# A decoder step with routed experts: the first LayerNorm's rows are reloaded unscaled and finished in the last stage, and more expert weights are prefetched

## The chip, the cores and the metric

The kernel runs on one core of one Trainium2 chip. The metric is the device time of one execution in microseconds (us), as the median of several runs; lower is better. The core has five engines, each with an instruction queue of its own: TensorE (PE, matmuls; its weight loads are shown as PEld), VectorE (DVE), ScalarE (ACT), GpSimd (POOL) and SyncE (SP). Sixteen DMA engines serve all queues. Here SP issues almost all weight loads, and a transfer that SP has to wait for holds up everything that SP issues behind it.

## The reference

One layer of a hybrid decoder for 512 prompt rows and 32 sample rows (8 sequences of 4 tokens), all in float32, model width 1024. The mixers (a matrix memory, sliding-window attention, their projections and gates) come first and are not touched by the change. What matters here stands behind them:

```
x = layer_norm(DN_ALPHA * x + mix, ln_g[0], ln_b[0])                        # LN1
x = layer_norm(DN_ALPHA * x + hier_moe(x, ...), ln_g[1], ln_b[1])           # LN2
ple = jax.nn.sigmoid(x @ w_pg) * (p_i @ w_pp)
x = layer_norm(DN_ALPHA * x + ple, ln_g[2], ln_b[2])                        # LN3
```

`hier_moe` routes each row: the best of 4 groups, and in it the best 2 of 8 experts, whose outputs are added with weights. An expert is `silu(x @ w_eg) * (x @ w_eu) @ w_ed`, with w_eg and w_eu of 1024 x 512 and w_ed of 512 x 1024, 6 MiB together. LN1's output x is needed three times: by the router, by the experts, and in the residual sum of LN2. Its scale and shift (ln_g[0], ln_b[0]) are the last step of it.

## The kernel before, in words

**Order of the work.** The mixers end with the output projection, a stream of matmuls over weights that pass through a staging pool on the right side of SBUF. Then come LN1 and the router's logits, the routing (some 17 us of short VectorE operations, with TensorE computing the embeddings `p_i @ w_pp` in between), the expert stage (`expert_phase`, written with semaphores by hand), and the last stage: LN2, the gate projection with `w_pg`, and LN3, one tile of 128 rows after the other (`moe_norm`, `turn`, `embed_norm`), with the 32 sample rows handled apart (`moe_norm_q`, `embed_norm_q`). Within a stage the compiler's scheduler orders the instructions, and `tc.issue_after` puts an instruction behind another. `expert_phase` is a critical section: the engines enter it when what they share has landed, and leave it together (L164), when each has signalled `fin`.

**LN1's rows.** `ln_scale` normalises a tile of rows in place in `r_p` (or `r_s` for the sample rows) without scale and shift, and SP writes it to `x1d` in DRAM. The router and the experts fold scale and shift into their own weights or into the copies behind the transposes, and read `x1d`. For LN2's residual sum, VectorE also multiplies by the gain and adds the shift in place (`ln_affine`, L1689, and `affine` inside the expert stage, L429), two operations a tile, and SP writes those rows to a second array `x1a`. The rows have to leave `r_p`, because it is the place of one expert's w_ed.

**The expert stage.** Four slots hold one expert's weights each: 2 MiB for the first half of gate and up (semaphore `gu`), 2 MiB for the second (`gv`), and 2 MiB for down in two halves (`wd`, `we`). The rows of an expert are worked on in items of 32. The slot of an expert is refilled as TensorE is done with its parts (`gh`, `gu`, `dn`), by a loop on SP that goes through the experts in order (L127 gate and up, L133 down). Some parts of the first four experts are loaded before the stage (`prefetch(slot, which)`); the rest at its start: SP issues a part of slot 3 and slot 2 there, between the writes of `x1a`, and waits for these writes (`xo`) where they leave the place `r_p` to w_ed. When an expert is the last in its slot, SP loads what the last stage needs into the place (`late`, L215): in this order of slots, rows of LN1 into slot 3's `r_p`, half of `w_pg` into slot 0, and the rows of ln_g and ln_b (`gb_rows`) into slot 1.

**The start of the last stage.** GpSimd gathers the two expert outputs of each row from `ybuf` (`gather`). TensorE spreads gains and shifts of LN2 and LN3 over the partitions: a matmul of one identity column, broadcast, with `gb_rows`, 512 columns at a time, and ScalarE copies the result out (`spread`, L2014 and L2015, eight matmuls). ScalarE and VectorE split `w_pg` into two parts (`split_from`). Then `moe_norm(0)` and `turn(0)` (transposes) come, and so on.

## Time and profile before

| what | value |
|---|---|
| median of 3 runs | 1167.32 us (1164.56 to 1167.94) |
| the profiled execution's own time | 1164.36 us |
| its span, from the first to the last instruction | 1162.6 us |
| TensorE busy | 90% of the span, mean granted clock 0.962 |
| VectorE, ScalarE, GpSimd busy | 42%, 28%, 20% |
| moved by DMA | 280.06 MB, mean 241 GB/s |

The span is shorter than the execution's time by what lies around it. Shares of busy time are averages over stages with different limits; what a stage waits for is read from its own windows. A matmul's end is modelled, so a busy TensorE is not one at its peak. [...]

### The profile page before, as it was taken

What the parts mean: (1) busy time and instruction counts of PE and PEld (TensorE: products, weight loads), DVE (VectorE), ACT (ScalarE), POOL (GpSimd) and SP (SyncE); (2) the same over time, 40 slices, a digit from 0 to 9 for tenths busy, and PEclk for the clock granted to TensorE, in tenths of its full rate; (3) what the DMA queues carried; (4) which work ended last, traced back from release to release, by engine and by line L of the source; (5) the groups of instructions that cost most, each with busy time, mean ns of one, the idle gap of its engine ahead of it and who ended that gap; (6) DMA issues with size and microseconds to landing.
All of it is one profiled execution on the core that took longest, in us unless ns stands there. A gap on an engine that the chain in (4) does not pass through costs nothing.

```text
span 1162.6 us, 26684 instructions
## 1 busy us (share of the span) xinstructions
PE 1042.6 (90%) x10267; PEld 810.4 (70%) x10268; DVE 494.1 (42%) x1244; ACT 324.0 (28%) x663; POOL 232.5 (20%) x325
## 2 busy tenths in 40 slices
PE   6999999999999999999999884685998979985986
PEld 6988999999877779889988442342555535542665
DVE  3645533456545546465565620110111111111796
ACT  4411223232554745233212210110222112211411
POOL 4000001301445553104200210110121101111421
PEclk9999999999999999999999998988999989998798
DMA  8542543335214434563496799999999999998901
GB/s 253 145 132 62 156 120 98 78 94 157 71 48 149 130 110 139 167 179 101 160 414 246 289 368 414 418 423 415 421 417 417 417 418 421 415 418 332 341 19 59
DMA packets 113751, 280.06 MB, mean 241 GB/s; under 512 B 15478, under 2 KB 71644, under 8 KB 99824
## 3 DMA queue, kind: packets, MB, share of 16 engines
q1 hardware_dynamic: 92704, 240.06, 55.3%
q0 software_dynamic: 15280, 33.59, 8.3%
q10 hardware_dynamic: 5696, 5.43, 1.5%
q8 instruction: 48, 0.79, 0.3%
q14 instruction: 23, 0.19, 0.1%
HBM read 249.21 MB, written 31.80 MB: 242 GB/s over the span
## 4 chain that ended last, share of the span: by engine, by line
PE 65%; DMA 13%; SPq 12%; DVE 5%; issue 4%; POOL 1%; ACT 0%; ACTq 0%; DVEq 0%; POOLq 0%
PE pj L611 13%; PE pj L613 13%; PE pj L612 12%; PE psG L282 7%; SPq L127 7%; DMA gu<-in_w_eu_dram 4%; SPq L133 4%; DMA w2b<-in_w_eu_dram 4%; PE psY L296 4%; PE tp L1220 2%; DMA x1a<-r_p 1%; PE sp L1266 1%; PE nm L1254 1%; DMA raw<-in_w_a_dram 1%; PE sp L671 1%
## 5 line engine op out<-in xcount | busy, mean ns | idle before, releaser
L611 PE MATMUL pj<-xH,wH 128*128 128x256 f32 (+1 forms) x672 | 198.2, 295 | 0.0
L613 PE MATMUL pj<-xH,wL 128*128 128x256 f32 (+1 forms) x672 | 197.6, 294 | 0.0
L612 PE MATMUL pj<-xL,wH 128*128 128x256 f32 (+1 forms) x672 | 195.8, 291 | 0.0
L524 ACT CAST wH<-raw 128x1024 fp32r<-128x1024 f32 x76 | 79.6, 1048 | 235.9 <-PE pj L612 149.0
L611 PEld LDWEIGHTS pj<-xH,wH 128*128 128x128 f32 x672 | 126.5, 188 | 6.3 <-issue 4.9
L613 PEld LDWEIGHTS pj<-xH,wL 128*128 128x128 f32 x672 | 126.5, 188 | 4.7 <-issue 4.3
L612 PEld LDWEIGHTS pj<-xL,wH 128*128 128x128 f32 x672 | 127.1, 189 | 2.7 <-issue 2.2
L525 DVE TENSOR_TENSOR wL<-raw,wH 128x1024 fp32r<-128x1024 f32 x76 | 94.9, 1249 | 72.6 <-ACT wH L524 71.9
L282 PE MATMUL psG<-w,xT 128*32 128x256 f32 x1216 | 78.2, 401 | 29.2 <-DMA w<-in_w_eu_dram 15.8
L386 ACT ACTIVATE sg<-psG 128x128 f32<-128x128 f32 x50 | 13.9, 278 | 288.2 <-PE psG L282 288.2
L282 PE MATMUL psG<-gu,xT 128*32 128x256 f32 x1088 | 70.7, 403 | 24.4 <-DMA gu<-in_w_eu_dram 18.3
L417 DVE COPY hT<-psH 128x128 f32<-128x128 f32 x50 | 14.6, 292 | 182.6 <-PE psH L287 182.6
L282 PEld LDWEIGHTS psG<-w,xT 128*32 128x32 f32 x1216 | 40.3, 114 | 58.2 <-issue 38.0
L282 PEld LDWEIGHTS psG<-gu,xT 128*32 128x32 f32 x1088 | 35.9, 114 | 50.9 <-issue 29.1
L246 POOL DMA_DIRECT2D ybuf<-ysb x50 | 35.1, 704 | 149.9 <-DVE ysb L424 145.8
L1242 POOL TENSOR_SCALAR lg<-lg,sm 128x256 f32<-128x256 f32 (+1 forms) x64 | 56.0, 888 | 28.6 <-DVE sm L1239 17.4
L412 DVE COPY xT<-xg 128x256 f32 (+1 forms) x50 | 14.7, 294 | 102.1 <-PE psG L282 101.8
L373 ACT ACTIVATE xg<-psX,gcol 128x128 f32 (+1 forms) x100 | 36.4, 468 | 47.0 <-PE psX L275 47.0
L282 PE MATMUL psG<-w2a,xT 128*32 128x256 f32 x448 | 32.2, 427 | 19.1 <-DMA w2a<-in_w_eu_dram 14.1
L611 PE MATMUL pj<-wH,xH 128*128 128x256 f32 x160 | 47.4, 296 | 0.0
L613 PE MATMUL pj<-wH,xL 128*128 128x256 f32 x160 | 44.9, 280 | 0.0
L612 PE MATMUL pj<-wL,xH 128*128 128x256 f32 x160 | 44.8, 280 | 0.0
(578 smaller groups left out, 2188.5 us busy)
## 6 DMA issues: line engine op xcount, KB each, us to landing
w<-in_w_eg_dram SPq DMA_DIRECT2D x28, 1024.0 KB, 22.6
w<-in_w_eu_dram SPq DMA_DIRECT2D x28, 1024.0 KB, 24.3
w<-in_w_ed_dram SPq DMA_DIRECT2D x28, 1024.0 KB, 25.3
raw<-in_w_in_dram SPq DMA_DIRECT2D x22, 1024.0 KB
w2b<-in_w_ed_dram SPq DMA_DIRECT2D x14, 1024.0 KB, 25.0
gu<-in_w_eg_dram SPq DMA_DIRECT2D x12, 1024.0 KB, 23.7
gu<-in_w_eu_dram SPq DMA_DIRECT2D x12, 1024.0 KB, 26.1
r_p<-in_w_ed_dram SPq DMA_DIRECT2D x12, 1024.0 KB, 22.9
```

Of the source, the lines that this page charges most:

```text
L127: return [eng.dma_start(out=W[s][half][:, i], in_=w[i][bass.ds(e, 1)].rearrange("a (p k) f -> (a p) k f", p=P)[:, ks]) for i in range(2)]
L133: return eng.dma_start(out=W[s][2][:, ks], in_=w[2][bass.ds(e, 1)].rearrange("a (k p) d -> p (a k) d", p=P)[:, ks])
L246: gp.dma_start(out=ybuf[bass.ds(i1 * 32, 32)].rearrange("t (c d) -> c t d", c=4), in_=ysb[:, r]).then_inc(S[f"y{r}"], 16)
L282: m = pe.matmul(psG[32 * q:32 * q + 32], xT[:, k], W[s][half][:, :, kh, P * q:P * q + P], start=k == 0, stop=k == KD - 1)
L296: m = pe.matmul(psY[32 * q:32 * q + 32], hT[:, 32 * k:32 * k + 32], W[s][2][:, k, 256 * q:256 * q + 256], start=k == 0, stop=k == 3)
L373: m = act.activation(out=out, in_=psX[:, k], func=AF.Identity, bias=gcol[:, 1, k:k + 1], scale=gcol[:, 0, k:k + 1])
L524: act.copy(out=H, in_=src)
L525: return eng.tensor_tensor(out=L, in0=src, in1=H.bitcast(F32), op=ALU.subtract)
L611: pe.matmul(out, lh(k), rh(k), start=start and i == 0, stop=False)
L612: pe.matmul(out, lh(k), rl(k), start=False, stop=False)
L613: pe.matmul(out, ll(k), rh(k), start=False, stop=stop and i == len(ks) - 1)
L1242: gp.tensor_scalar(out=lg[:, par, j, 0:nk], in0=lg[:, par, j, 0:nk], scalar1=sm[:, 2, par, j:j + 1], scalar2=None, op0=ALU.mult)
```

## The change

- `x1a` and all writes of it go. `late` reloads all four tiles of rows from `x1d`, unscaled, in the expert stage's end (semaphore `rb`); before, one came back there and three in the last stage. VectorE's scale and shift of these rows move behind the experts: two tiles at the end of the expert stage, one early in the last stage, one (and the sample rows) in the middle of it.
- The two tiles `w2b` and `gu3` (8 rows of 1024 a partition each) become four of half the size, so that each waits for its own part of the staging pool alone. Of the first four experts everything but the second half of slot 3's gate and up is prefetched before the stage: 3 MiB more than before. SP's issues at the stage's start shrink to that one pair.
- Four of the six spreads (LN1's and LN2's gains and shifts, eight matmuls) are made inside the expert stage, by TensorE behind its last matmul, with ScalarE copying; LN3's two stay in the last stage.
- Small index and weight computations move from the last stage into the routing. Two runs of idle matmuls stand in the last stage, six become eight in the routing. The second half of `w_pg` is issued behind the first gather's landing. `moe_norm_q` and `embed_norm_q` come earlier.

```diff
-def expert_phase(tc, pool, psum, ident, meta, tok, x1, W, w, ybuf, spare, gcol, gb, xs, xa, late, warm):
...
+def expert_phase(tc, pool, psum, ident, meta, tok, x1, W, w, ybuf, spare, gcol, late, rows, spreads, xs, any_):
...
-        def rows_out(t):
-            sp.dma_start(out=xa[t * P:(t + 1) * P], in_=xs[t]).then_inc(S["xo"], 16)
-
-        rows_out(0)
         for d in load_gu(sp, W, NB - 1, w, NB - 1, 1):
             d.then_inc(S[f"gv{NB - 1}"], 16)
-        sp.wait_ge(S["xo"], 16)
-        load_dn(sp, W, NB - 1, w, NB - 1, 0).then_inc(S[f"wd{NB - 1}"], 16)
-        for t in (1, 2):
-            sp.wait_ge(S["af"], 2 * t)
-            rows_out(t)
-        load_dn(sp, W, NB - 2, w, NB - 2, 1).then_inc(S[f"we{NB - 2}"], 16)
-        sp.wait_ge(S["xo"], 48)
-        load_dn(sp, W, NB - 1, w, NB - 1, 1).then_inc(S[f"we{NB - 1}"], 16)
...
-                        for out, src in late[s]:
-                            sp.dma_start(out=out, in_=src).then_inc(S["al"], 16)
+                        for out, src, name in late[s]:
+                            sp.dma_start(out=out, in_=src).then_inc(S[name], 16)
...
-        sp.wait_ge(S["al"], 16 * sum(len(loads) for loads in late))
+        of = lambda which: 16 * sum(name == which for loads in late for _, _, name in loads)
+        sp.wait_ge(S["al"], of("al"))
...
-        for s in range(NB - 1):
-            for n in ("wd", "we")[:1 + (s < NB - 2)]:
+        for s in range(NB):
+            for n in ("wd", "we"):
...
+        halves = [(n, out[:, 512 * i:512 * (i + 1)], which, slice(512 * i, 512 * (i + 1))) for n, (out, which) in enumerate(spreads)
+                  for i in range(2)]
+        banks = [psX[:, 4 * i:4 * i + 4].rearrange("p k t -> p (k t)") for i in range(2)]
+        pe.wait_ge(S["gr"], 32)
+        for n, (_, _, which, cs) in enumerate(halves):
+            if n > 1:
+                pe.wait_ge(S["sc"], n - 1)
+            pe.matmul(banks[n % 2], ident[0:6, which:which + 1].to_broadcast([6, P]), rows[:, cs], start=True, stop=True).then_inc(S["se"], 1)
...
+        for n, (_, out, _, _) in enumerate(halves):
+            act.wait_ge(S["se"], n + 1)
+            act.copy(out=out, in_=banks[n % 2]).then_inc(S["sc"], 1)
+        act.wait_ge(S["sc"], len(halves))
...
-        def affine(t, i):
-            if i:
-                dve.wait_ge(S["af"], 2 * t - 1)
-            dve.tensor_tensor(out=xs[t], in0=xs[t], in1=gb[:, i], op=(ALU.mult, ALU.add)[i]).then_inc(S["af"], 1)
-
-        affine(1, 0)
...
-        affine(1, 1)
-        affine(2, 0)
-        affine(2, 1)
...
+        dve.wait_ge(S["rb"], of("rb"))
+        for i, op in enumerate((ALU.mult, ALU.add)):
+            dve.wait_ge(S["sc"], 2 * i + 2)
+            if i:
+                dve.wait_ge(S["ra"], len(xs))
+            for x in xs:
+                dve.tensor_tensor(out=x, in0=x, in1=spreads[i][0], op=op).then_inc(S["ra"], 1)
+        dve.wait_ge(S["ra"], 2 * len(xs))
...
+    spart = stg.tile([P, 256], F32, name="spart", bufs=1)
...
-    w2b = WB.tile([P, 8 * D], F32, name="w2b")
-    w_tiles[2] = (w_tiles[2][0], halves_of(w2b[:, 0:4 * D])[0], w2b[:, 4 * D:].rearrange("p (k d) -> p k d", k=4), None)
-    gu3 = WB.tile([P, 8 * D], F32, name="gu3")
-    w_tiles.append((*halves_of(gu3), r_p, None))
-
-    wpp, pT = gu3[:, 4 * D:6 * D].rearrange("p (k d) -> p k d", k=2), gu3[:, 6 * D:6 * D + 2 * NG].rearrange("p (k s) -> p k s", k=2)
+
+    gu3a, gu3b, w2b, w2d = (WB.tile([P, 4 * D], F32, name=name) for name in ("gu3a", "gu3b", "w2b", "w2d"))
+    w_tiles[2] = (halves_of(w2a)[0], halves_of(w2b)[0], w2d[:].rearrange("p (k d) -> p k d", k=4), None)
+    w_tiles.append((halves_of(gu3a)[0], halves_of(gu3b)[0], r_p, None))
+    for _ in prefetch(2, (1,)):
+        pass
+
+    wpp, pT = gu3b[:, 0:2 * D].rearrange("p (k d) -> p k d", k=2), gu3b[:, 2 * D:2 * D + 2 * NG].rearrange("p (k s) -> p k s", k=2)
...
-    gb1 = ln_consts(w_tiles[2][2][:, 2:4], 0, act)
-    for _ in prefetch(2, (1,)):
-        pass
-    next(prefetch(2, (2,)))
...
-    def ln_affine(t, parts=(0, 1)):
...
-    def x1_out(t):
-        sy.dma_start(out=x1a[t * P:t * P + x1s[t].shape[0]], in_=x1s[t])
...
-        logit = dve.tensor_tensor(out=lgt[:rows, t], in0=pl[:rows, t], in1=brr[:rows], op=ALU.add)
-        if t in (1, 2):
-            with tc.issue_after(logit.ins):
-                ln_affine(NT, (t - 1,))
-    for _ in prefetch(3, (0,)):
-        pass
-    x1_out(NT)
+        dve.tensor_tensor(out=lgt[:rows, t], in0=pl[:rows, t], in1=brr[:rows], op=ALU.add)
+    for s, which in ((2, 2), (3, 0), (3, 2)):
+        for _ in prefetch(s, (which,)):
...
-        PL = pool("pl", bufs=4, stack=scope)
+        PL = pool("pl", bufs=3, stack=scope)
...
-        with tc.issue_after(tokens.ins):
-            ln_affine(0)
-            x1_out(0)
-            ln_affine(1)
+
         idle = rps([P, 512], "pj", 2)
         with tc.issue_after(product.ins):
-            for _ in range(6):
-                pe.matmul(idle[:, 0:256], ident, keep[:, 0:256], start=True, stop=True)
+            for _ in range(8):
+                product = pe.matmul(idle[:, 0:256], ident, keep[:, 0:256], start=True, stop=True)
+        with tc.issue_after(tokens.ins):
+
+            dve.tensor_scalar(out=wsum, in0=wts[:, 1], scalar1=1.0, scalar2=ALPHA, op0=ALU.add, op1=ALU.mult)
...
+            pq = rps([P, 4], "nm")
+            with tc.issue_after(product.ins):
+                pe.matmul(pq, same[:NS].rearrange("p q t -> p (q t)"), smp4, start=True, stop=True)
...
-    gain2, shift2, gain3, shift3 = (row(W1, i) for i in range(4))
-
-    gb_rows = row(W1, 4)[0:4]
-    gbq = row(W1, 4).rearrange("p (i j d) -> p i j d", i=2, j=2)
+    gain1, shift1, gain2, shift2 = (row(W1, i) for i in range(4))
+    gain3, shift3 = row(W1, 11), row(w2a, 2)
+
+    gb_rows = row(W1, 4)[0:6]
+
...
-    r_back = lambda t: (r_p[:, t], x1a[t * P:(t + 1) * P])
+    r_back = lambda t: (r_p[:, t], x1d[t * P:(t + 1) * P])
     late = [
-        [pg_half(0)],
-        [(gb_rows[2 * j:2 * j + 2], A[n][0, 1:3]) for j, n in enumerate(("ln_g", "ln_b"))],
+        [(*pg_half(0), "al")],
+        [(gb_rows[3 * j:3 * j + 3], A[n][0], "gr") for j, n in enumerate(("ln_g", "ln_b"))],
         [],
-        [r_back(0)],
+        [(*r_back(t), "rb") for t in range(NT)],
     ]
+    spreads = [(gain1, 0), (shift1, 3), (gain2, 1), (shift2, 4)]
...
+    def keep_busy(n, behind=None):
+
+        idle = ps2.tile([P, 256], F32, name="pp", bufs=1)
+        with tc.issue_after(behind.ins) if behind else nullcontext():
+            for _ in range(n):
+                m = pe.matmul(idle, ident, keep[:, 0:256], start=True, stop=True)
+        return m
+
+    def affine(x, gain, shift):
+        dve.tensor_tensor(out=x, in0=x, in1=gain, op=ALU.mult)
+        return dve.tensor_tensor(out=x, in0=x, in1=shift, op=ALU.add)
...
-        return ln_apply(x2, stats, gain2, shift2)
+        if t:
+            return ln_apply(x2, stats, gain2, shift2)
+        for half in range(2):
+            cs = slice(512 * half, 512 * (half + 1))
+            first = ln_apply(x2[:, cs], stats, gain2[:, cs], shift2[:, cs])
+        return first
...
+        affine(x1q, gbq[0][:, 0], gbq[0][:, 1])
...
     gather(1)
 
-    for out, src in (pg_half(1), r_back(1), (embeds[:, 0:512], pld[P:2 * P, 512:]), r_back(2), (embeds[:, 512:512 + D], pld[2 * P:3 * P]),
...
-        sy.dma_start(out=out, in_=src)
-    spreads = chain(spread(gain2, 0), spread(shift2, 2), spread(gain3, 1), spread(shift3, 3))
+    for n, (out, src) in enumerate((pg_half(1), (embeds[:, 0:512], pld[P:2 * P, 512:]), (embeds[:, 512:512 + D], pld[2 * P:3 * P]),
+                                    (embeds[:, 512 + D:], pld[3 * P:4 * P]), (pls, plsd[:]),
+                                    (x1q, x1d[SEQ:].rearrange("t (q d) -> q t d", q=4)))):
+        with tc.issue_after(first.ins) if n else nullcontext():
+            dma = sy.dma_start(out=out, in_=src)
+        if n == 0:
+            first = dma
+            tc.add_manual_dep(dma.ins, landed.ins.name, mybir.DependencyInfo(mybir.DependencyClass.Sync, mybir.DependencyReason.DATA),
+                              reason="behind the first rows")
+    busy = keep_busy(8)
     for k in range(KD):
-        copied = next(spreads) if k >= 4 else None
-        with tc.issue_after(copied.ins) if copied else nullcontext():
-            split_from(pg(k, 0, 0, 512), pg(k, 1, 0, 512), pg_in[0][:, k])
-    for copied in spreads:
-        pass
-
-    idle = ps2.tile([P, 256], F32, name="pp", bufs=1)
-    with tc.issue_after(spread_last["ins"].ins):
-        for _ in range(6):
-            pe.matmul(idle, ident, keep[:, 0:256], start=True, stop=True)
+        cast = split_from(pg(k, 0, 0, 512), pg(k, 1, 0, 512), pg_in[0][:, k])
+    with tc.issue_after(busy.ins), tc.issue_after(cast.ins):
+        third = affine(x1s[2], gain1, shift1)
+        spread(gain3, 2)
+        busy = spread(shift3, 5)
+    keep_busy(8, busy)
...
+    with tc.issue_after(third.ins):
+        behind, applied = moe_norm(0)
...
-            with tc.issue_after(applied.ins if t > 1 else lows.ins):
-                if t < NT:
+            if t < NT:
+                with tc.issue_after(applied.ins if t > 1 else lows.ins):
+                    if t == NT - 1:
+                        affine(x1s[t], gain1, shift1)
                     behind, applied = moe_norm(t)
-                else:
+            if t == NT - 2:
+                with tc.issue_after(applied.ins):
                     moe_norm_q()
-        if t > NT:
-            embed_norm_q()
+            if t == NT:
+                embed_norm_q()
```

## Rows read from the trace of the kernel before

**Rows 1.** Window of 100 us: length, busy times, PE clock, DMA share, GB/s.
```profile
800.00:900.00 100.00, 87.42 (x1394) 50.10 (x1390) 17.06 (x57) 20.33 (x50) 14.69 (x22) 0.97 1.02 419
```

**Rows 2.** DMA issues of SP as the expert stage starts.
```profile
681.59 0.38 SPq L133 DMA_DIRECT2D r_p<-in_w_ed_dram  x1
684.45 0.37 SPq L127 DMA_DIRECT2D w<-in_w_eg_dram  x1
```

**Rows 3.** Timeline of TensorE, first items.
```profile
668.16 3.66 PE L282 MATMUL psG<-w,xT 128*32 128x256 f32 x64
...
679.98 1.91 PE L296 MATMUL psY<-w,hT 128*32 128x256 f32 x32
...
711.66 3.64 PE L282 MATMUL psG<-w,xT 128*32 128x256 f32 x32 [7.50 <-DMA w<-in_w_eu_dram]
```

**Rows 4.** Waits of SP, 655 to 1067 us: total, times, longest.
```profile
SPq L164 <- DMA xg<-x1d,tok: 3.6, 1, 3.6
...
SPq L164 <- DMA x1a<-r_p: 1.0, 1, 1.0
```

**Rows 5.** Timeline of VectorE behind the routing.
```profile
653.47 4.62 DVE L1689 TENSOR_TENSOR r_p<-r_p,w2b 128x1024 f32<-128x1024 f32 x4
```

**Rows 6.** A window of 4 us behind the prefetches of the routing.
```profile
652.00:656.00 4.00, 3.35 (x18) 1.72 (x18) 3.60 (x8) 0.00 (x0) 2.37 (x3) 1.00 0.46 175
```

**Rows 7.** Late DMA issues of SP as the expert stage ends.
```profile
1045.03 0.42 SPq L215 DMA_DIRECT2D r_p<-x1a  x1
1050.23 0.39 SPq L215 DMA_DIRECT2D w<-in_w_pg_dram  x1
1062.42 0.31 SPq L215 DMA_DIRECT2D w<-in_ln_g_dram  x1
```

**Rows 8.** Windows behind the last expert matmuls.
```profile
1068.00:1069.00 1.00, 0.00 (x0) 0.00 (x0) 0.00 (x0) 0.00 (x0) 0.54 (x1) 1.00 0.39 150
...
1071.00:1072.00 1.00, 0.00 (x0) 0.00 (x0) 0.00 (x0) 0.00 (x0) 0.00 (x0) 0.50 0.02 8
```

**Rows 9.** Timeline of TensorE from the last expert matmul on.
```profile
1064.69 1.93 PE L296 MATMUL psY<-w2b,hT 128*32 128x256 f32 x32 [1.01 <-DVE hT L417]
1072.84 13.98 PE L2014 MATMUL po<-w,keep 4*128 4x512 f32 x16 [6.22 <-SPq L164]
...
1086.76 5.00 PE L2117 MATMUL pp<-keep 128*128 128x256 f32 x12
...
1091.59 1.04 PE L2034 MATMUL tp<-keep,r_p 128*128 128x128 f32 x8
...
1134.79 1.03 PE L2034 MATMUL tp<-keep,r_p 128*128 128x128 f32 x8
```

**Rows 10.** Windows while TensorE runs spreads, then idle matmuls.
```profile
1080.00:1084.00 4.00, 4.00 (x5) 1.40 (x5) 2.31 (x4) 2.24 (x4) 0.00 (x0) 0.50 1.04 420
...
1088.00:1092.00 4.00, 4.00 (x14) 3.21 (x14) 1.28 (x1) 0.00 (x0) 3.37 (x3) 0.61 1.01 411
```

**Rows 11.** Timelines of VectorE, GpSimd, ScalarE, and one chain line.
```profile
1067.85 3.85 DMA ybuf<-ysb
...
1073.53 1.03 POOL L1999 DMA_INDIRECT w<-ybuf,yidx  x1 [4.99 <-SPq L164]
...
1075.27 1.88 DVE L525 TENSOR_TENSOR pg<-w,pg 128x512 fp32r<-128x512 f32 x3
...
1083.74 1.28 DVE L2020 SCALAR_TENSOR_TENSOR r_p<-w,wts,r_p 128x1024 f32<-128x1024 f32 x1 [0.68 <-DMA w<-ybuf,yidx]
...
1086.86 0.59 ACT L2015 COPY w<-po 128x512 f32<-128x512 f32 x1 [1.12 <-PE po L2014]
...
1092.85 1.29 DVE L2036 TENSOR_TENSOR xT<-tp,xT 128x512 fp32r<-128x512 f32 x2 [3.12 <-issue]
...
1128.88 1.27 DVE L1683 SCALAR_TENSOR_TENSOR r_p<-r_p,lmv,w 128x1024 f32<-128x1024 f32 x1
```

90 lines of the change are left out of this document (40 added, 50 removed).

## The prediction

> **What bounds the kernel now.** I read the page first, then windows over the whole span, and then, for the stages that the change touches, SP's queue, TensorE's timeline, the waits and the windows again in fine steps. Through the expert stage the DMA engines are full: in the window shown, and in the others from 690 to 1060 us, their share is 1.02 at about 419 GB/s, while TensorE is at 87% [rows 1]. TensorE waits there for weights, not the weights for TensorE. So that stage is a stream of bytes: it ends earlier by what its start comes earlier and by what is taken out of it. Behind it the bound changes: the end of the stage waits for a store, the start of the last stage for gathers, VectorE and a TensorE at half clock, and its rest for VectorE and TensorE in turn.
>
> **Part 1: the stream of weights starts earlier.** Before, slot 0's second expert is first asked for at 684.45 us, because SP stood until 681.59 waiting for the writes of LN1's rows, and then read its registers for 2.5 us (684.45 less 681.59 and 0.38) [rows 2]. Now SP has one pair to issue at some 663.5 us and is at that point by about 667.5. What then holds it is TensorE: the first 32 of the 64 matmul records of the first item are through at 668.16 + 3.66/2 = 670.0, the others at 671.8 [rows 3]. So 4 MiB (4.19 MB) are asked for at 670 to 672 us, and take 10.0 us at 419 GB/s. The down part is free at 679.98 + 1.91 = 681.9 [rows 3], just as these are through. From there the queue never empties. When the old stream started, 684.45, the new one is ahead by those 10.0 us and by 684.45 - 681.9 = 2.5 us: 12.5. TensorE can't take all of it at once: its second item in slot 1 waited only 7.5 us [rows 3]. What it can't take stays in the queue as lead, and the next items wait for their own landings again, so the last weights land 12.5 us earlier.
>
> To this comes the entry into the stage. It waited for the first gather, and then 1.0 us more for a write of `x1a` [rows 4]. Without the write it can begin some 0.8 us earlier, behind the gather and the index matmul moved there. Together **13.3 us** off. Bounds: 10 (entry 2 us later through more traffic, the down part 1 us later) and 15 (the gather lands another 1.5 us earlier, as four VectorE operations of 4.62/4 = 1.16 us that stood behind the token list are gone [rows 5]).
>
> The prefetches that make it possible cost no time where they land before the entry. By the sizes they put about 2 MB more into the time in front of it (3 MiB of weights, less 1 MiB of gains and shifts), 5 us at 419 GB/s, and the old queue ran empty inside 652 to 656 us [rows 6]: some 658 us, in front of an entry at 661.5. If that cover is gone, each us is a us. The small operations moved into the routing stand behind the token list and in front of the same gather: nothing, bound 0.5 us.
>
> **Part 2: the end of the stage gets longer.** This is the term that I think is easily overlooked. The spreads now run behind the last expert matmul, which ends at 1064.69 + 1.93 = 1066.6 (times of this part are before's; all of them move by part 1), and the stage isn't left until all eight are copied. They need `gb_rows`, which SP asks for last, at 1062.42, behind the rows at 1045.03 and 2 MiB of `w_pg` at 1050.23 [rows 7]. Before, this queue is through by 1068.4: the DMA share falls to 0.39 in that us, and what follows is the last store [rows 8]. Now three more tiles of rows, 1.57 MB, are in front: 3.75 us, so 1072.1, and 1.3 us until the semaphore is seen, an estimate between 0.5 and 3: 1073.4.
>
> By then TensorE has been idle for 6.8 us. Its granted clock is down to 0.50 from 1071 on in the same idle time of before [rows 8], and the eight spreads of before, begun cold at 1072.84, took 13.98 us, with the clock at 0.50 in the window shown and in its neighbours [rows 9, 10]. I take the same 13.98 us. Then come the last copy, 0.59 [rows 11], and the way out of the stage, 0.9 (before, the last store landed at 1067.85 + 3.85 = 1071.7, and the spreads began 1.1 later [rows 9, 11]). 1073.4 + 14.0 + 0.6 + 0.9 = 1088.9, against 1072.8: **16.1 us** on. Behind TensorE's new wait for `gb_rows` stand only the spreads and its `fin`, but ScalarE, VectorE, SP and GpSimd all wait for these. The four VectorE operations on two tiles, 4 x 1.16 [rows 5], and the reload of the rows are hidden under the spreads; if the spreads were short, they would be next, at about 1076 us. Bounds: 15 and 18 by the landing; 11.4 if the clock rises (a rival).
>
> [...]
>
> **Part 3: the last stage begins quicker.** Before, from the stage's end at 1072.8, the first transposes start at 1091.59, 18.8 us later, and the second half of `turn(0)` is through at 1092.85 + 1.29 = 1094.1, 21.3 later [rows 9, 11]. Eight spreads and idle matmuls to 1091.8 kept TensorE until then [rows 9], and the second gathered tile landed at 1083.7, among 2 MiB of `w_pg` and three tiles of rows [rows 11]. Now four spreads are left, and `w_pg`'s second half waits for the gather. SP's new wait for that gather holds the other half of `w_pg`, the embeddings and the sample rows behind it; at 419 GB/s the 2 MiB of `w_pg` take 5 us and are there by some +15, in front of the splits that need it at +18, and the rest is needed later: nothing, bound 1 us. VectorE is what sets the pace: from +1.0 it has eight subtractions of 1.88/3 = 0.63 (5.0), then the third tile's two operations (2.3): +8.3. The gathered tiles should be there by +8 (the first is issued at +0.7 [rows 11]). The first sum takes 1.2, to +9.5. From the second sum to the first transposes it was 1091.59 - 1083.74 = 7.85, with about 1.9 of waiting for idle matmuls in it: 5.95. The halves of tile 0 save 0.6: transposes at +14.9, and the second half through at +17.9. **3.4 us** off; bounds 1 (the tiles land as late as before) and 4.5.
>
> Behind it, work is only reordered up to the fourth tile. VectorE gains two operations (2.3 us) and the sample rows' part, which I estimate at 4 us from its operations on a quarter of the columns, in front of the fourth tile's LN2. That ended at 1128.88 + 1.27 = 1130.15, and TensorE turned to it at 1134.79 [rows 9, 11]: 4.6 us of cover for 6.4. The 1.8 us left over can be filled by the sample rows' matmuls, which now come earlier. I take nothing, bounds -1.7 and +4.6.
>
> **The sum.** -13.3 + 16.1 - 3.4 = -0.6 us, on the profiled execution's 1164.36: 1163.8. The median of the runs is 2.96 above that execution, so in its terms 1166.7. About 0.3% (3.5 us) is what a measurement of this kernel can tell from no change.
>
> **Rivals.**
> - *The clock rises under the spreads* (0.14). For it: idle matmuls of 128 rows, begun at 1086.76 at the same half clock, had it at full by about 1091, as the window's mean of 0.61 shows [rows 9, 10]. Against it: 14 us of 4-row matmuls didn't. If it rose as late as there, 2.5 spreads would run at 1.75 us and 5.5 at half of that: 9.2 instead of 14.0, and the time is 1161.9.
> - *`gb_rows` lands before TensorE is done* (0.05), because small transfers get past the large ones. The spreads then follow warm, 7 us, and the rows' operations end the stage near 1076: part 2 is 3.5, and the time 1154.
> - *The favourable ends add up* (0.13): the stage entered 1.5 us earlier, the matmuls of the sample rows in a gap (-1.7), tiles landing early (-1): 1162.5.
> - *VectorE becomes late in the middle of the last stage* (0.13), the one on the other side. If the fourth tile's LN2 is late by all of 6.4 us behind a scheduler's order that puts the sample rows first, the 4.6 us of cover are needed elsewhere and TensorE stands: +4.6, 1171.3. It decides from 4.1 us on.
> - *The stage isn't entered earlier* (0.09), so that the change doesn't do what it says: the place of slot 3's down part is free only when the rows' writes are out, and these now queue behind more weights. If its 2 MiB land at 665 instead of 658, the entry is 4 us later than I count: 1170.7. It decides from 661.5 on.
>
> **How the numbers follow.** The forecast, no change that can be told, has 0.46, with 1166.7 and 1163.2 to 1170.2 of its own. The first three rivals are faster by more than 0.3%, 0.32; the last two slower, 0.22. The range leaves out about one in ten on either side: 1158 (early entry together with a rising clock) to 1171.5.
>
> **What would show it.** Part 1: SP asks for slot 0's second expert near 670 us, and TensorE's last expert matmuls start near 1051.4 instead of 1064.69. Part 2: eight spreads of some 14 us at a clock of 0.50 between the last expert matmul and the first gather, that begin 6 to 7 us after TensorE's last. Part 3: first transposes 15 us behind the stage's end. I am wrong if the spreads run at 1.00, if they begin right behind the last matmul, or if the stream starts later than 673 us.

## The result: 0.6% slower

The changed kernel takes 1174.74 us (median of 16 runs, 1169.1 to 1176.77), the kernel before 1167.39 beside it (16 runs): a ratio of 1.0058 (95%: 1.0044 to 1.0073), which is 6.8 us of 1167.39, and outside the range that was given. Its profiled execution is the median one: own time 1174.74, span 1173.1. That is 10.5 us above the span of before; as before's profiled execution is 3 us below its median, sums made between these two executions come out some 3 us too high.

Two views of SP in the changed kernel come first: its issues around the stage's start and end, and the wait that was new (total, times, longest).

```profile
668.14 0.36 SPq L127 DMA_DIRECT2D w<-in_w_eg_dram  x1
...
1053.88 1.69 SPq L202 DMA_DIRECT2D w<-in_ln_g_dram  x1
1055.61 0.39 SPq L202 DMA_DIRECT2D w<-in_ln_b_dram  x1
1089.17 0.40 SPq L2119 DMA_DIRECT2D w<-in_w_pg_dram  x1
```
```profile
SPq L2119 <- DMA w<-ybuf,yidx: 8.1, 2, 7.5
```

Slot 0's second expert is asked for at 668.14, 16.3 us earlier than in [rows 2] (forecast 670). From there on the transfer engines stay busy, as foreseen: in windows of 2 us from 672 to 700 us their share is 0.97 or more. Windows of the changed kernel, in the expert stage and behind it (length, busy times, TensorE's clock as a share of full speed, DMA share, GB/s):

```profile
800.00:900.00 100.00, 93.20 (x1531) 53.39 (x1527) 18.87 (x63) 20.92 (x51) 16.07 (x24) 1.00 1.02 410
1062.00:1064.00 2.00, 0.00 (x0) 0.00 (x0) 0.00 (x0) 0.00 (x0) 0.00 (x0) 0.50 0.59 219
1066.00:1081.00 15.00, 14.01 (x16) 4.97 (x16) 4.72 (x4) 4.69 (x8) 0.00 (x0) 0.50 0.00 0
```

The first one answers to [rows 1], and this is the line that the prediction didn't have: the DMA share is 1.02 as before, but what these full engines moved is 410 GB/s, not 419. It is so through the whole stage (413 from 720 to 800 us, 412 from 900 to 1050). TensorE's timeline of the same kernel, from the last expert matmul on, answers to [rows 9]:

```profile
1056.15 1.93 PE L284 MATMUL psY<-w2d,hT 128*32 128x256 f32 x32 [1.01 <-DVE hT L418]
1066.35 14.01 PE L360 MATMUL psX<-w,keep 6*128 6x512 f32 x16 [8.26 <-DMA w<-in_ln_b_dram]
1081.73 5.58 PE L2017 MATMUL pp<-keep 128*128 128x256 f32 x16 [1.37 <-SPq L163]
1087.25 3.77 PE L2008 MATMUL po<-w,keep 6*128 6x512 f32 x8
...
1096.44 1.32 PE L2046 MATMUL tp<-keep,r_p 128*128 128x128 f32 x8 [1.77 <-DVE r_p L1676]
...
1114.68 1.94 PE L2046 MATMUL tp<-keep,r_p 128*128 128x128 f32 x8 [5.46 <-DVE r_p L1676]
```

From slot 0's request to the last expert matmuls it was 1064.69 - 684.45 = 380.2 us before and is 1056.15 - 668.14 = 388.0 now. The stage's weights therefore end 8.5 us earlier, not 13.3. Behind them TensorE waits 8.26 us for the rows of ln_g and ln_b, and the eight spreads take 14.01 us at a clock of 0.50. The last stage starts 1081.73 - 1056.15 = 25.58 us behind the last expert matmuls, before 1072.84 - 1064.69 = 8.15: 17.4 on, forecast 16.1. The first transposes stand 14.7 us behind the last stage's start, forecast 14.9. The whole last stage is 1173.1 - 1081.73 = 91.4 us long, before 1162.6 - 1072.84 = 89.8: 1.6 on, where 3.4 off was forecast. Sum: -8.5 + 17.4 + 1.6 = 10.5.

What lowers the rate? In the middle of the stage the engines do the same transfers of the same sizes, but into other places of SBUF, where each tile of weights has 128 partitions. Part of the change, seen above only as its uses, moves small tiles out of and into the pool `const`, which lies in front of the large ones:

```diff
-    trib = const.tile([P, P], BF16, name="trib")
-    oneb = const.tile([P, P], BF16, name="oneb")
-    one = const.tile([P, 2, NEXP], F32, name="one")
-    lgt = const.tile([P, NT5, NGRP + NEXP], F32, name="lgt")
+    trib = RC.tile([P, P], BF16, name="trib")
...
+    wsum = const.tile([P, NT5], F32, name="wsum")
+    yidxq = const.tile([P, 2], I32, name="yidxq")
+    smpq = const.tile([P, 4], F32, name="smpq")
+    same = const.tile([P, 4, NS], F32, name="same")
+    quarter = const.tile([P, 4], F32, name="quarter")
+    which = const.tile([P, 4], F32, name="which")
```

By the addresses in the two built programs, 832 bytes a partition less lie in front of `r_p`, `w0`, `w1` and `w2a`. Before, these began at bytes 12544, 29952, 79104 and 128256 of each partition, all 256 past a multiple of 512; now at 11712, 29120, 78272 and 127424, all 64 short of one. The tiles on the right side (`w2b`, `w2d`, `gu3a`, `gu3b`; before `w2b`, `gu3`) begin 480 past a multiple of 512 in both kernels.

### The profile page after: what moved, and what is told of

Same layout as the page of the kernel before. It is cut to its first block, busy times and chain, and to the rows that moved or that the text cites. A ratio compares the mean times of both kernels' runs of the same rounds, so it can differ in the third digit from the quotient of the medians.

```text
span 1173.1 us, 26748 instructions
## 1 busy us (share of the span) xinstructions
PE 1051.4 (90%) x10299; PEld 816.5 (70%) x10300; DVE 493.3 (42%) x1246; ACT 326.6 (28%) x667; POOL 229.1 (20%) x325
## 4 chain that ended last, share of the span: by engine, by line
PE 64%; DMA 16%; SPq 12%; DVE 5%; issue 2%; ACT 0%; POOL 0%; DVEq 0%; ACTq 0%; POOLq 0%
PE pj L612 13%; PE pj L614 12%; PE pj L613 12%; SPq L127 8%; DMA w2b<-in_w_eu_dram 6%; PE psG L270 6%; DMA gu3b<-in_w_eu_dram 4%; SPq L133 3%; PE psY L284 3%; PE tp L1221 2%; PE sp L1267 1%; PE nm L1255 1%; PE psX L360 1%; DMA raw<-in_w_a_dram 1%; PE sp L672 1%
## 5 line engine op out<-in xcount | busy, mean ns | idle before, releaser
L270 PE MATMUL psG<-w,xT 128*32 128x256 f32 x1216 | 74.8, 387 | 22.6 <-issue 11.7
L383 ACT ACTIVATE sg<-psG 128x128 f32<-128x128 f32 x50 | 13.9, 278 | 281.3 <-PE psG L270 281.3
L418 DVE COPY hT<-psH 128x128 f32<-128x128 f32 x50 | 14.6, 292 | 170.9 <-PE psH L275 170.9
L413 DVE COPY xT<-xg 128x256 f32 (+1 forms) x50 | 14.7, 295 | 109.7 <-PE psG L270 109.4
L270 PE MATMUL psG<-gu3a,xT 128*32 128x256 f32 x544 | 35.9, 407 | 20.9 <-DMA gu3a<-in_w_eu_dram 14.9
L270 PEld LDWEIGHTS psG<-gu3a,xT 128*32 128x32 f32 x544 | 19.5, 116 | 35.3 <-issue 29.1
## 6 DMA issues: line engine op xcount, KB each, us to landing
w<-in_w_ed_dram SPq DMA_DIRECT2D x28, 1024.0 KB, 25.2
r_p<-in_w_ed_dram SPq DMA_DIRECT2D x12, 1024.0 KB, 23.4
```

The source lines that it names most:

```text
L270: m = pe.matmul(psG[32 * q:32 * q + 32], xT[:, k], W[s][half][:, :, kh, P * q:P * q + P], start=k == 0, stop=k == KD - 1)
```

## The experiments

Medians in us, with the ratio to the kernel before, run on the same chip beside them. "To stage" goes from the start of the last expert matmuls to the last stage's first matmul, and "last stage" from there to the span's end; these and the rate are of one profiled execution. No kernel here leaves out a part of the computation.

| run | median | ratio (95%) | GB/s, 800 to 900 us | to stage | last stage |
|---|---|---|---|---|---|
| before | 1167.39 | | 419 | 8.2 | 89.8 |
| after | 1174.74 | 1.0058 (1.0044 to 1.0073) | 410 | 25.6 | 91.4 |
| e0, one run | 1165.86 | | 419 | 8.1 | 89.7 |
| e4 | 1168.23 | 0.9993 (0.9977 to 1.0009) | 418 | 25.2 | 92.4 |
| e5 | 1175.1 | 1.0058 (1.0042 to 1.0074) | 412 | 8.2 | 90.1 |
| e8 | 1165.25 | 0.9968 (0.9951 to 0.9985) | 420 | 21.8 | 91.9 |
| e2 | 1166.63 | 0.9982 (0.9964 to 1.0001) | 411 | 14.6 | 91.9 |
| e3 | 1181.61 | 1.0102 (1.0076 to 1.0129) | 411 | 31.0 | 93.2 |
| e6 | 1163.94 | 0.9962 (0.9949 to 0.9975) | 411 | 10.6 | 93.4 |
| e1 | 1177.39 | 1.0068 (1.0043 to 1.0093) | 411 | 24.5 | 93.7 |
| e11 | 1175.27 | 1.0061 (1.004 to 1.0081) | 411 | 23.9 | 92.2 |
| e7 | 1177.34 | 1.0065 (1.0046 to 1.0085) | 412 | 24.0 | 91.7 |
| e12 | 1164.66 | 0.9976 (0.9958 to 0.9994) | 420 | 22.6 | 92.9 |
| e15 | 1164.03 | 0.9975 (0.9961 to 0.9989) | 420 | 23.4 | 88.3 |
| e9 | 1153.81 | 0.9867 (0.984 to 0.9895) | 420 | 10.6 | 92.2 |

### Where the weights lie (e0, e4, e5, e8)

e0 is the kernel before, unchanged, to see how far its stream's rate repeats.

> The kernel before, unchanged, for its weight stream. The changed kernel's stream ran at 410 to 413 GB/s in the windows from 720 to 1050 us, that of before at 418 to 419; over 360 us that is some 6 us. If the change slows the stream, this run shows 418 to 419 again, while the changed kernel's relatives run with it show 410 to 413. The rival, that the rate belongs to the chip or the run, gives the same rate in all kernels of this call.

e4 is the changed kernel with one tile 64 bytes longer, of which the old part alone is used. The instructions stay the same; `r_p`, `w0`, `w1` and `w2a` now begin at multiples of 512.

```diff
-    meta = const.tile([1, P], I32, name="meta")
+    meta = const.tile([1, P + 16], I32, name="meta")[:, 0:P]
```

> The changed kernel, instruction by instruction the same, with one small tile in front of the weights' places made 64 bytes longer: r_p, w0, w1 and w2a then begin at a multiple of 512 bytes in each partition, where the change had put them 64 bytes short of one (before: 256 past one). Theory: the stream of weights is slower by 1.7% since the change because of where its places begin; the rate rises from 410 to 413 GB/s to 418 to 420, the last expert matmul comes 6 us earlier, and the time is some 1168.5. Rival: the rate goes with the order or the number of the transfers in flight, which this leaves as it is: 410 to 413, 1174 to 1175.

e5 is the kernel before with the same tile 64 bytes shorter (its last columns aren't read), so that the four tiles begin 192 past a multiple of 512 instead of 256. One copy of that tile gets shorter with it; all else stays.

```diff
-    meta = const.tile([1, P], I32, name="meta")
+    meta = const.tile([1, P - 16], I32, name="meta")
...
-        dve.tensor_copy(out=meta, in_=mf)
+        dve.tensor_copy(out=meta, in_=mf[:, 0:P - 16])
```

> The counterpart in the kernel before: the same small tile made 64 bytes shorter, so that its r_p, w0, w1 and w2a begin 192 bytes past a multiple of 512 and no longer 256; every instruction is kept. Theory: its stream falls from 418 to 420 GB/s to 410 to 413 and it gets 6 us slower, some 1173.5. Rival: nothing changes, 1167.5.

The same window of e0, e5 and e4, a line each:

```profile
800.00:900.00 100.00, 89.11 (x1394) 50.47 (x1390) 16.89 (x56) 19.36 (x49) 14.39 (x22) 0.95 1.02 419
```
```profile
800.00:900.00 100.00, 86.66 (x1330) 48.92 (x1326) 15.96 (x53) 16.14 (x40) 12.01 (x18) 0.91 1.02 412
```
```profile
800.00:900.00 100.00, 93.11 (x1524) 53.35 (x1520) 18.51 (x61) 20.91 (x51) 16.07 (x24) 1.00 1.02 418
```

Compare the last two columns: the share is 1.02 in all, the bytes differ. 64 bytes one way take the loss off the changed kernel (1.0058 to 0.9993), 64 bytes the other way put the same loss on the kernel before (1.0058). From slot 0's request to the last expert matmuls it is 380.4 us in e0 and 380.5 in e4, but 386.5 in e5, 387.0 in e1 and 388.2 in e2, which lie as the changed kernel does; e4's two ends:

```profile
668.59 0.36 SPq L127 DMA_DIRECT2D w<-in_w_eg_dram  x1
...
1049.08 1.93 PE L284 MATMUL psY<-w2d,hT 128*32 128x256 f32 x32 [1.01 <-DVE hT L418]
```

That is the cause of the loss: with the places moved back, the changed kernel can't be told from the one before.

e8 moves the right side too, by a tile of 480 bytes behind the others in their pool, on top of e4: all destinations of weights now begin at multiples of 512.

> The changed kernel with both moves: the small tile 64 bytes longer, as in the run before, and 480 bytes left free behind the other group of weights' places (gu3a, gu3b, w2b, w2d), which in every kernel so far began 480 bytes past a multiple of 512. All places then begin at a multiple of 512, and every instruction is kept. A third of the weights goes into that group. If it is as slow as the rest was at 448, 1/418.5 = (2/3)/F + (1/3)/411.5 gives F = 422 GB/s for places that begin at a multiple: the stream runs at 422, 0.9% less of some 365 us, and the time is 1165. Rival: this group's place plays no part, 418 to 419, 1168.

In the windows below, of e8, the rate is 422 and 420 GB/s, and the kernel is 0.32% faster than before. Its interval overlaps e4's, and the way to the last expert matmuls is 380.6 us, as in e4; what comes earlier is the end of the queue, the spreads' rows, 387.0 us behind slot 0's request and not 390.3:

```profile
720.00:800.00 80.00, 58.51 (x797) 30.50 (x792) 9.64 (x32) 10.60 (x26) 8.06 (x12) 0.82 1.02 422
800.00:900.00 100.00, 93.31 (x1519) 53.15 (x1515) 18.08 (x60) 20.92 (x51) 16.05 (x24) 0.99 1.02 420
```

So the runs agree: in the windows from 720 to 900 us the rate is 410 to 413 GB/s where the four tiles on the left begin 448 or 192 past a multiple of 512 (the changed kernel, e5), 418 to 420 where they begin at 256 or 0 (before, e0, e4), all of these with the right side at 480, and 420 to 422 where all begin at 0 (e8). From 421 to 411 GB/s, between e8 and the changed kernel, it is 2.4%. Why a place costs rate, and whether it is the writing into SBUF that does it, no run shows.

### The end of the expert stage (e2, e3, e6)

The prediction put 14 us for the spreads down to a cold start. e2 asks for the rows of ln_g and ln_b earlier, into `gu3a`, where slot 3's first gate half is done with, so that the spreads follow the last expert matmul without a wait. e3 leaves the rows late and lets TensorE run idle matmuls until they land.

```diff
+    gb_early = gu3a[0:6, 0:D]
...
-        [(gb_rows[3 * j:3 * j + 3], A[n][0], "gr") for j, n in enumerate(("ln_g", "ln_b"))],
+        [(gb_rows[3 * j:3 * j + 3], A[n][0], "al") for j, n in enumerate(("ln_g", "ln_b"))],
         [],
-        [(*r_back(t), "rb") for t in range(NT)],
+        [(gb_early[3 * j:3 * j + 3], A[n][0], "gr") for j, n in enumerate(("ln_g", "ln_b"))]
+        + [(*r_back(t), "rb") for t in range(NT)],
...
-                     x1d[:], w_tiles, w_e, ybuf[:], spare, gcol8, late, gb_rows, spreads, x1s[:2],
+                     x1d[:], w_tiles, w_e, ybuf[:], spare, gcol8, late, gb_early, spreads, x1s[:2],
```

> The changed kernel with the six rows of gains and shifts for the spreads at the stage's end loaded about 20 us earlier, into slot 3's gate tile, so that the spreads need not wait 8.3 us for them. Theory: they start right behind the last expert matmul. If TensorE then keeps the clock that it has there, they take 7 us and the stage ends 15 us earlier, some 1160; if the spreads themselves let the clock fall, they take up to 14 and the stage ends 8 us earlier, some 1166.5. Rival: the queue of transfers is what is late, and the rows land no earlier: 1174, no change.

```diff
-        pe.wait_ge(S["gr"], 32)
+        [pe.matmul(psG[:].rearrange("p i f -> p (i f)"), ident, any_, start=True, stop=True) for _ in range(36)]; pe.wait_ge(S["gr"], 32)
```

> The changed kernel with 36 idle matmuls of 128 rows and 256 columns between the last expert matmul and the wait for the gains' rows (about 8 us of work in a wait of 8.3). Theory: the eight spreads take 14.0 us because they start at the granted clock of 0.50 that the idle time has left; started warm they take 7 us, and the time is some 1167.7. Rival: matmuls of 6 rows run slow, or bring the clock down, whatever stood before them: 14 us again, 1174 to 1176.

Timelines of TensorE in e2, then in e3, and e3's windows around the first spreads:

```profile
1058.26 1.93 PE L284 MATMUL psY<-w2d,hT 128*32 128x256 f32 x32 [1.01 <-DVE hT L418]
1060.12 11.38 PE L360 MATMUL psX<-gu3a,keep 6*128 6x512 f32 x16
```
```profile
1062.34 15.81 PE L356 MATMUL psG<-keep 128*128 128x256 f32 x72
1078.08 11.98 PE L360 MATMUL psX<-w,keep 6*128 6x512 f32 x16
```
```profile
1078.00:1080.00 2.00, 2.00 (x6) 0.79 (x6) 0.00 (x0) 0.59 (x1) 0.00 (x0) 1.00 0.00 0
1080.00:1082.00 2.00, 2.00 (x4) 0.77 (x4) 1.22 (x2) 1.02 (x2) 0.00 (x0) 0.58 0.00 0
1082.00:1084.00 2.00, 2.00 (x4) 0.73 (x3) 1.25 (x3) 0.74 (x2) 0.00 (x0) 0.50 0.00 0
```

e2 takes the wait away, 11 us of the stage's end, and with it the loss (0.9982), at the low rate of the stream still. But a warm start isn't enough: in e2 the spreads take 11.38 us, in e3 11.98. In e3 TensorE was busy without a gap, first with idle matmuls of 128 rows, then with spreads of 6 rows, and its clock went from 1.00 to 0.50 under the spreads. The idle matmuls took longer than was planned, 15.81 us at a clock of 1.00, which is why e3 is the slowest of all.

So the spreads themselves let the clock fall. e6 is e2 with one difference: each spread reads all 128 partitions. The identity's column is zero but for the one row, so what is added is old weights times zero.

```diff
-            pe.matmul(banks[n % 2], ident[0:6, which:which + 1].to_broadcast([6, P]), rows[:, cs], start=True, stop=True).then_inc(S["se"], 1)
+            pe.matmul(banks[n % 2], ident[:, which:which + 1].to_broadcast([P, P]), rows[:, cs], start=True, stop=True).then_inc(S["se"], 1)
...
-    gb_early = gu3a[0:6, 0:D]
+    gb_early = gu3a[:, 0:D]
```

> The kernel with the gains' rows loaded early, with spreads that read all 128 partitions (the other 122 rows of the tile are old weights and are multiplied by zeros): the same 16 matmul records with the same columns. Theory: matmuls of 4 or 6 rows let the granted clock fall to 0.50 some 2.5 us after they begin, however warm TensorE was; with 128 rows it stays at 1.00, and the spreads take 7 us instead of 11.4: 1162.3. Rival: the clock falls because the matmuls are few and wait for the copies, whatever their rows: 11.4 again, 1166.6.

TensorE's timeline in e6, and one of its windows under the spreads:

```profile
1061.02 7.38 PE L360 MATMUL psX<-gu3a,keep 128*128 128x512 f32 x16
```
```profile
1066.00:1068.00 2.00, 2.00 (x6) 0.59 (x4) 1.90 (x3) 1.37 (x3) 0.00 (x0) 1.00 0.14 48
```

7.38 us at a clock of 1.00 throughout, for the same columns. Between e2 and e6 the spreads differ in nothing but the rows that they read: with 6 the clock fell to 0.50, with 128 it stayed. The fall isn't seen in every run of six-row spreads: the four of the changed kernel's last stage, 3.77 us behind idle matmuls, end at 1.00 (windows from 1087 to 1091 us).

### The last stage (e1, e7, e11, e12, e15)

The half of `w_pg` that now waits for the first gather was to be there by +15. SP stood 7.5 us for that gather and asked at +7.4 (1089.17), and ScalarE saw the rows at +18.2. The sample rows' work stands in front of the fourth tile, as VectorE's timeline of the changed kernel shows below ScalarE's:

```profile
1099.88 4.26 ACT L2145 CAST pg<-w 128x512 fp32r<-128x512 f32 x8 [1.49 <-DMA w<-in_w_pg_dram]
```
```profile
1139.43 0.27 DVE L1662 BATCH_NORM_AGGREGATE lmv<-pp 128x2 f32<-128x24 f32 x1 [3.49 <-PE pp L2086]
```

e1 puts the sample rows behind the last tile again, as before; e11 puts `moe_norm_q` behind the fourth tile (`t == NT - 1`) and leaves the rest.

```diff
-            if t == NT - 2:
+            if t == NT:
                 with tc.issue_after(applied.ins):
                     moe_norm_q()
-            if t == NT:
-                embed_norm_q()
+        if t > NT:
+            embed_norm_q()
```

> The changed kernel with the sample rows' LN2 and their embedding gate back where the kernel before issues them (last), all else kept. Theory: VectorE comes late in the last stage because the sample rows' operations stand in its queue in front of the fourth tile's LN2, one of them waiting 3.5 us for TensorE; so the stage from its first gather to the end, 91.4 us in the changed kernel, falls to 85 to 87 and the time from 1174.7 to some 1169.5. Rival: the last stage is set by what starts late in it (gathers, splits, VectorE's sum of work), and the order is worth 1 us at most: 1174.

> The changed kernel with one thing moved: the sample rows' LN2 is issued behind the fourth tile's LN2 and no longer in front of it; their embedding gate stays in front of the third tile's. Theory: the fourth tile's LN2, which ends 69.5 us behind the stage's start (57.4 before), comes some 9 us earlier, and TensorE, which stands for 9 us between the third and the fourth tile's transposes or does the sample rows' matmuls there, gets 3 us of it back: 1171.5. Rival: the order costs nothing, since the sample rows' work only changes places with the tile's, as it did when it went last: 1174 to 1177.

Neither gains: the last stage is 93.7 and 92.2 us. Yet both bring the fourth tile forward. Its transposes, in the changed kernel and in e11:

```profile
1151.42 1.10 PE L2046 MATMUL tp<-keep,r_p 128*128 128x128 f32 x8
```
```profile
1142.28 1.03 PE L2046 MATMUL tp<-keep,r_p 128*128 128x128 f32 x8
```

Behind the stage's start that is 69.7 us and 61.4 (61.0 in e1); before, it was 62.0 [rows 9]. So the sample rows do hold the fourth tile back by some 8 us, but with them behind it the stage ends no sooner: their place in the order isn't what the length hangs on. e7 takes work out of the last stage instead: all four tiles get scale and shift in the expert stage, under the spreads.

```diff
-                     x1d[:], w_tiles, w_e, ybuf[:], spare, gcol8, late, gb_rows, spreads, x1s[:2],
+                     x1d[:], w_tiles, w_e, ybuf[:], spare, gcol8, late, gb_rows, spreads, x1s[:NT],
...
-        third = affine(x1s[2], gain1, shift1)
...
-    with tc.issue_after(third.ins):
-        behind, applied = moe_norm(0)
+    behind, applied = moe_norm(0)
...
-                    if t == NT - 1:
-                        affine(x1s[t], gain1, shift1)
```

> The changed kernel with the gain and shift of LN1 put on all four tiles of rows at the end of the expert stage, where VectorE waits for the spreads, and not on two there and two in the last stage. Theory: VectorE sets the pace of the last stage (busy for 76.9 us of 91.4, against 72.8 of 89.8 before), so the four operations of 1.18 us that it is rid of there are saved, 4.7 us: 1170. Rival: TensorE has 4.6 us of slack that hides them and the order of the operations decides: 1173.5 to 1174.7.

TensorE's timeline in e7 shows what came in place of it:

```profile
1098.27 6.21 PE L2017 MATMUL pp<-keep 128*128 128x256 f32 x16
1104.32 1.04 PE L2046 MATMUL tp<-keep,r_p 128*128 128x128 f32 x8
```

VectorE was through with the first tile's LN2 at 1098.90 + 1.42 = 1100.3; the transposes waited 4 us more, for idle matmuls that ran at half clock for the most part (0.50 from 1098 to 1102 us). e12 (on top of e8, with e7's edit) leaves these out, and e15 also lets SP ask for the second half of `w_pg` at once.

```diff
-    keep_busy(8, busy)
```

> The kernel with all places at a multiple of 512 (1165.25), gain and shift of LN1 on all four tiles inside the expert stage under the long spreads, and without the second eight idle matmuls of the last stage. Theory: VectorE's sum of work sets the last stage, and where its four operations went into the stage alone, the 4.7 us came back as TensorE's idle matmuls at a clock of 0.50, which held the first transposes back until 4 us behind the first tile's LN2; without them the transposes come at some 13.5 us into the stage and the stage takes 87 us instead of 91.9: 1160.5. Rival: TensorE then starts the first products cold and loses there what it gained: 1164 to 1165.

```diff
-            tc.add_manual_dep(dma.ins, landed.ins.name, mybir.DependencyInfo(mybir.DependencyClass.Sync, mybir.DependencyReason.DATA),
-                              reason="behind the first rows")
```

> The kernel with LN1's gain and shift on all four tiles in the expert stage and without the second idle matmuls (1164.7), with the second half of the gate's weights asked for at once. There the splits stood 6.5 us for it, from 15.8 to 22.3 us into the stage. Theory: it is this half that kept VectorE's 4.7 us from showing; asked for 7.5 us earlier, the splits start at 16 us, and 5 to 6 us are saved: 1159. Rival: the gathers come later by as much, and VectorE's first sums with them: 1163 to 1165.

ScalarE in e12, then VectorE in e15:

```profile
1094.95 4.27 ACT L2142 CAST pg<-w 128x512 fp32r<-128x512 f32 x8 [6.56 <-DMA w<-in_w_pg_dram]
```
```profile
1080.86 1.28 DVE L2026 SCALAR_TENSOR_TENSOR r_p<-w,wts,r_p 128x1024 f32<-128x1024 f32 x1 [2.46 <-DMA w<-ybuf,yidx]
```

Each wait was followed by the next. Without the idle matmuls, ScalarE stood 6.56 us for `w_pg`; with `w_pg` asked for at once, the gathers came later, and VectorE stood 2.46 us for them: its first sum starts 8.4 us into the stage (1080.86 less 1072.42), in e12 4.9 (1078.23 less 1073.29). e15's profiled execution has the shortest last stage of all, 88.3 us, but its median is only 0.6 us below that of e12.

### The parts together (e9, e10, e13, e14, e16, e17)

e9 puts e8's places and e6's spreads into the changed kernel.

> Both moves of the places together with the gains' rows loaded early and spreads that read 128 rows. If the gains add up, 1163.9 for the rows and the spreads, less 6.5 for the first move, less 3 for the second: 1154.5 (1157.5 if the second gives nothing). Rival: a stage that ends earlier meets the rows' transfers at its end, and part of it is given back: 1160.

Its timeline of TensorE at the stage's end:

```profile
1049.31 1.93 PE L284 MATMUL psY<-w2d,hT 128*32 128x256 f32 x32 [1.01 <-DVE hT L418]
1051.18 7.39 PE L360 MATMUL psX<-gu3a,keep 128*128 128x512 f32 x16
1059.94 3.69 PE L2019 MATMUL pp<-keep 128*128 128x256 f32 x16 [1.37 <-SPq L163]
```

The last stage starts 12.9 us earlier than in [rows 9], and the kernel takes 1153.81 us against 1168.44 beside it: 1.3% faster than before, and by the two ratios 1.9% faster than the changed kernel. No other run is measurably faster. Five tried to improve its last stage:

| run | edit on e9 | median | ratio (95%) | last stage |
|---|---|---|---|---|
| e10 | all rows finished in the expert stage, sample rows behind the fourth tile | 1157.58 | 0.9903 (0.9874 to 0.9933) | 91.6 |
| e13 | the third tile's scale and shift behind the first tile's LN2 | 1156.53 | 0.9899 (0.9875 to 0.9923) | 93.1 |
| e14 | the second half of `w_pg` asked for at once | 1153.9 | 0.9896 (0.9873 to 0.992) | 90.4 |
| e16 | e13 and e14 together | 1156.06 | 0.9905 (0.989 to 0.9919) | 94.0 |
| e17 | the second half of `w_pg` loaded in the expert stage | 1158.95 | 0.9931 (0.9914 to 0.9948) | 91.6 |

> As the last one, with gain and shift of LN1 put on all four tiles in the expert stage, and the sample rows' LN2 issued behind the fourth tile's and no longer in front of it. Theory: both stand in VectorE's queue in front of the fourth tile's LN2, and only together do they hold TensorE up; the fourth tile's transposes come 10 us earlier in the stage, and 4 to 6 us are saved. Rival: TensorE's slow start in the last stage (its idle matmuls and spreads at a clock of 0.50) sets the rest, and nothing or 1 us is saved.

> The fastest so far (1153.8) with one thing moved: the third tile's gain and shift (2.4 us on VectorE) are issued behind the first tile's LN2 and no longer in front of it. Theory: VectorE sets the pace of the last stage from its first microsecond, and TensorE waits 3.7 us for the first tile's LN2: the first transposes come 2 us earlier, VectorE fills its wait for them with the third tile, and 1.5 to 2.4 us are saved: 1152. Rival: VectorE's sum is the same, so the second tile's LN2 comes when it came before: 1153.8.

> The fastest so far (1153.8) without the changed kernel's new dependency: SP asks for the second half of the gate's weights at the last stage's start, as before, and not behind the first gather. Theory: this half lands too late for the splits (they stand 1.5 us for it, at 18 to 19 us into the stage), and behind that wait lies all that VectorE has been rid of: here it is worth 1.5 us at most, 1152.5, since VectorE is busy until shortly before. Rival: the gathers, which it now shares the transfer engines with, land later, and the first tile's LN2 with them: 1155 to 1157.

> The kernel with the third tile's gain and shift issued behind the first tile's LN2 (1156.5), with the second half of the gate's weights asked for at once. VectorE stood 4.8 us for it there. Theory: 3 to 4.8 us are saved: 1152. Rival: the gathers come later by as much: 1156.

> The fastest so far (1153.8) with the second half of the gate's weights loaded at the end of the expert stage, behind the first. Its 2 MiB take 5.0 us at 419 GB/s; the transfer engines run empty there at some 1056.5 us, so it lands at 1061.5, and the stage ends at 1062.6 and no longer at 59.9: 2.7 us later. Theory: the last stage then has neither this half nor its traffic among the gathers, and gets 3 to 4 us shorter, 1153. Rival: VectorE's work sets it anyway: 1156.5.

With short spreads nothing hides VectorE's eight operations. In e10 they run until 1064.3, 4 us behind the last copy of a spread:

```profile
1054.90 9.36 DVE L476 TENSOR_TENSOR r_p<-r_p,w 128x1024 f32<-128x1024 f32 x8 [2.16 <-DMA r_p<-x1d]
```

So the last stage starts 1065.03 - 1050.33 = 14.7 us behind the last expert matmuls, in e9 10.6. In e17 it is 16.0; there SP stands 3.8 us for the rows of ln_b, which land behind the second half of `w_pg`. e14 can't be told from e9.

## Why the prediction was wrong

The sum was -13.3 + 16.1 - 3.4 and came out as -8.5 + 17.4 + 1.6. Two terms failed, by about as much: the first by 4.8 us and the third by 5.0.

**Part 1, the step that failed first.** It took for granted that the stream keeps its rate: "take 10.0 us at 419 GB/s", and that the stage "ends earlier by what its start comes earlier and by what is taken out of it". The start came 16.3 us earlier, more than was said; but the weights then moved at 410 to 413 GB/s instead of 419, and the way from that request to the last expert matmuls got 7.8 us longer. 16.3 - 7.8 = 8.5 us off, in place of 13.3. With the places moved back by 64 bytes (e4) the last expert matmuls start at 1049.08, 15.6 us earlier than in [rows 9], and the ratio is 0.9993; the forecast of 1166.7 on 1167.3 is 0.9995. From the first to the last expert matmuls, which leaves the entry out, it was 396.5 us before and 396.1 in e0; it is 390.2 in the changed kernel and 382.6 in e4, which is 13.5 to 13.9 us off, where the prediction had 12.5 for the stream. So the mechanism of part 1 held, and what was missed is a cost that none of the rivals named, with the places of the weights as its cause. That e4 meets the forecast's ratio is luck in part: its last stage is 2.6 us longer, not 3.4 shorter. (e4's parts, read between single executions as above, give -15.6 + 17.0 + 2.6 = +4.0 us where its ratio says 0.8 off. A good part of this can lie ahead of the stage, where single executions of the same code differ by several us, as said under the entry.)

**Part 2: the size was right, the reason not.** 17.4 us were measured where 16.1 were forecast; the rows landed 8.26 us behind TensorE (6.8 forecast), the spreads took 14.01 (13.98 forecast) at 0.50. The 1.3 us until the semaphore is seen, in the forecast of the landing, were an estimate that no row shows; in the changed kernel the DMA share falls from 0.47 in the us from 1063 to 0.09 in that from 1065, and the spreads start at 1066.35. But "begun cold" was taken for the reason. Begun warm, six-row spreads take 11.4 to 12.0 us; with 128 rows 7.4. The rival *`gb_rows` lands before TensorE is done* would have given "warm, 7 us": e2 made that happen, and it was 11.38. The rival *the clock rises under the spreads* is out: the clock was at 0.50 for all 14 us.

**Part 3: the start was right, the rest not.** First transposes at +14.7 for +14.9. The step that failed is "I take nothing" behind them: it was +5.7, as they stand 4.1 us earlier in the last stage than before, and the stage is 1.6 longer. The lead lasts until the third tile's transposes (3.4 us) and is gone at the fourth's (7.7 us behind). The prediction put 6.4 us more in front of the fourth tile's LN2 and 4.6 of cover; it ended 69.5 us into the stage, not 57.3, which is 12.1 later. So the nearest rival is *VectorE becomes late in the middle of the last stage*: the fourth tile was late behind the sample rows, as it said, but e1 and e11, which take these away from there, get no shorter stage. A smaller miss is `w_pg`, "there by some +15 ... nothing, bound 1 us": it was seen at +18.2, because SP's wait for the gather lasted 7.5 us and the load 10.7 us, not 5, and the splits stood 1.5 us for it.

The longer stage doesn't come of a short profiled execution of before: there it is 89.8, 89.7 (e0) and 90.1 (e5), and 91.4 to 93.4 in the seven kernels here that keep the changed one's last stage (after, e2, e3, e4, e6, e8, e9). What sets its length stays open: other orders, less work, fewer idle matmuls and an earlier `w_pg` left it between 88.3 and 94.0 us.

**The entry** came 2.2 us earlier between the two profiled executions (0.8 forecast), by the first expert matmuls, which answer to [rows 3]; below them a window of the changed kernel just ahead of SP's first issue in the stage, at 661.04:

```profile
665.99 3.66 PE L270 MATMUL psG<-w,xT 128*32 128x256 f32 x64
```
```profile
660.00:662.00 2.00, 0.48 (x4) 0.51 (x5) 0.00 (x0) 0.00 (x0) 0.00 (x0) 1.00 0.00 0
```

One pair of executions can't show 0.8 us: in e0, the kernel before again, they start at 670.15, and in the kernels with the change, whose instructions are the same up to there, between 665.42 (e13) and 673.95 (e7). The reason that the rival *the stage isn't entered earlier* gave, prefetches that land late, is out in the profiled execution: the DMA share there is 0.00, so they had landed. That the entry is earlier at all isn't shown by one pair.

## What to carry to other kernels

When the DMA engines are the bound, read GB/s beside their share, and after any change of small tiles work out at which byte the large destinations begin: here 832 bytes taken away in front of the weights cost some 7 us, and a pad of 64 bytes gave them back (6.5 us by the medians, 7.6 by the ratios). A place is tested by itself with a small tile made longer or shorter by 64 bytes, with next to no instruction changed, on both kernels. A run of broadcasts by matmul that read a few rows is worth trying with all 128 read, the rest times zero, and with its rows there before TensorE falls idle: here this took the spreads from 14.0 to 7.4 us. And when the forecast is a sum of parts that nearly cancel, compare each part with its own measurement; the total can come out right by luck.
